# The causal mask of a stick-breaking attention: from an accumulating matmul to a table read by VectorE

## The chip, the core and the metric

The kernel runs on one core of one Trainium2 chip. The metric is device time in microseconds (us), the median of several executions. It computes two layers of a hybrid trunk on a sequence of 1024 tokens of width 1024, in float32 throughout; the large products are made of three matmuls each, of a high and a low part (`F32R`).

## The reference, cut to what matters

Each layer runs four token mixers side by side on one projection (attention, a state-space branch S5, retention, and a gated recurrence RG-LRU), gates them and projects back. The change touches the attention alone:

```python
def stick_breaking_attention(q, k, v):
    '''q, k, v: (B, H, S, d). A[t,s] = beta_ts * prod_{s<j<t} (1 - beta_tj), s < t only.'''
    ...
        z = jnp.einsum('bhqd,bhkd->bhqk', q[:, :, lo:hi], k[:, :, :hi])
        t_idx = lo + jnp.arange(Q_BLOCK)[:, None]
        s_idx = jnp.arange(hi)[None, :]
        mask = s_idx < t_idx
        log_fail = jnp.where(mask, jax.nn.log_sigmoid(-z), 0.0)
        after = lax.cumsum(log_fail, axis=3, reverse=True) - log_fail
        w = jnp.where(mask, jnp.exp(jax.nn.log_sigmoid(z) + after), 0.0)
        outs.append(jnp.einsum('bhqk,bhkd->bhqd', w, v[:, :, :hi]))
```

A weight is beta = sigmoid(z) of its own key, times the product of 1 - beta over the keys between it and the query. Keys at or after the query count as 1 in the product and get the weight 0. There are 4 heads of 64 channels and blocks of 128 queries.

## The kernel before, in words

The work is cut into four units: layer 0 and 1, and in each two halves of 512 tokens (`units`, pairs of layer l and half c). A unit is a list of 64 "tiles" of the big projections (`filler`): for each, a block of weights is loaded by DMA (`raw`), split by ScalarE (ACT) into a high part `wh` and by VectorE (DVE) into a low part `wl` (`split`, L106), and multiplied on TensorE (PE) into PSUM banks named `pa`. `ahead` splits half a tile at a time, three halves ahead of the one that PE is at; there are five buffers each for `wh` and `wl`. The projections' results are read out by ACT (sigmoid, `actv`, L83, or `copy`, L86) and DVE (`tt`, L89).

The token mixers are generators whose steps are put between the tiles by a fixed table (`PLAN`) or at fixed tiles; everything is issued in the order written, each engine works its own queue in that order, and the only thing that lets an engine go on is a semaphore. PSUM banks of the mixers are named `pb`, five in all. So PE always has projection matmuls to run between the mixers' small ones.

The attention is `sba`. It starts at tile 12 of a unit and takes two steps on every even tile. It has 16 jobs per unit: four blocks b of 128 queries, four heads h. A job's keys are cut into segments of at most 512 (`segs`): in the first half of the sequence one segment of w = 128, 256, 384 or 512 keys; in the second half one of 512 and one of 128 to 512. The last segment ends with the 128 keys of the block itself, where the mask lies. For a job i:

- first step: PE makes the logits of each segment with two matmuls (query high and low part against `kS`, L1035 and L1036). A segment of 128 keys is padded to 256 columns. In the last segment a third matmul (L1038) adds `identb` times `trib`, a 128x128 table of 0 and -1e30, to the last 128 columns: that is the mask. ACT takes two sigmoids, f = 1 - beta and `be` = beta.
- second step: DVE scans f from right to left with a running product (L1057) and multiplies `be` with it, shifted by one key. Where there are two segments, the carry goes over as `ec`, a product of two columns.
- first step of the next job: PE transposes the weights `be` in pieces of 128 (L1019), ACT copies each segment to `wt` (L86), and PE multiplies them with the values two jobs later.

The small copies to `identb` and `trib` stand in the main loop at L1439; `con` is the table of constants, loaded in `first`.

Of the kernel before, what the change touches and what calls it, by code (L numbers as in the profile page):

```python
# [24 lines left out]
EPS = 1e-6  # L25
BIG = -1e30
EXPSET = "natural_log_exp_and_others"
# [4 lines left out]

(K_ID, K_DEC, K_XI, K_ZETA, K_CD, K_TRI, NCON) = (
    0, 128, 640, 896, 900, 902, 1030)
HALF = (512, 640)
# [7 lines left out]
@with_exitstack  # L43
def hybrid_kernel(ctx: ExitStack, tc: tile.TileContext, x, xt, ws1, ws2, par, bcw, preg, postg, con, rot, out, dbg=None):
    nc = tc.nc
# [7 lines left out]
    parp = ctx.enter_context(tc.tile_pool(name="parp", bufs=1))  # L53
    smp = ctx.enter_context(tc.tile_pool(name="smp", bufs=3))
    genp = ctx.enter_context(tc.tile_pool(name="genp", bufs=NGEN))
    psa = ctx.enter_context(tc.tile_pool(name="psa", bufs=3, space=bass.MemoryType.PSUM))
# [5 lines left out]
    def nm(s):  # L62
        cnt[0] += 1
        return f"{s}{cnt[0]}"
# [60 lines left out]
    cdec = cons[:, K_CD:K_CD + 2]  # L125
    identb = const.tile([P, P], F32R, name="identb")
    trib = const.tile([P, P], F32R, name="trib")
    kS = [const.tile([P, SEQ], F32R, name=f"kS{h}") for h in range(4)]
# [215 lines left out]
    def first():  # L344
# [15 lines left out]
        load_to(3)  # L360
        sp.dma_start(cons[:, P:], con[:, P:])
        lru_load(0)

# [327 lines left out]
    def lru_load(l):  # L691
        S["lw"] = G()
        sp.dma_start(S["lw"][:, 0:256], bcw[l, :, 1024:1280])
# [194 lines left out]
    def ret(l, c):  # L888
# [70 lines left out]
        yield 0  # L959
        st = smp.tile([P, 64], F32, tag="rst", name=nm("rst"))  # L960
        mu, va, yv, av = (st[:, i * 16:(i + 1) * 16] for i in range(4))
# [27 lines left out]
    def sba(l, c):  # L989
# [9 lines left out]
        for i in range(n + 3):  # L999
# [14 lines left out]
            if 1 <= i <= n:  # L1014
                st = J[i - 1]
                for (o, w), r in zip(st["sg"], st["w"]):
                    ps = B()
                    for q in range(w // P):
                        pe.transpose(ps[:, q * P:(q + 1) * P], r[:, q * P:(q + 1) * P], ident)  # L1019
                    wt = G()  # L1020
                    copy(wt[:, 0:w], ps[:, 0:w])
                    Bdone()
                    st["wt"].append(wt)
                st["w"] = None
            if i < n:

                b, h = js[i]
                sg = segs(b)
                st = J[i] = dict(b=b, h=h, sg=sg, f=[], w=[], wt=[])
                qh, ql = S["q", b]  # L1030
                for k, (o, w) in enumerate(sg):
                    ps = B()
                    wp = max(w, 256)
                    last = k == len(sg) - 1
                    mm(ps[:, 0:wp], qh[:, h * P:(h + 1) * P], kS[h][:, o:o + wp], True, False)  # L1035
                    mm(ps[:, 0:wp], ql[:, h * P:(h + 1) * P], kS[h][:, o:o + wp], False, not last)  # L1036
                    if last:
                        mm(ps[:, w - P:w], identb, trib, False, True)  # L1038
                    f, be = G(), G()
                    actv(f[:, 0:w], ps[:, 0:w], AF.Sigmoid, scale=-1.0)  # L1040
                    actv(be[:, 0:w], ps[:, 0:w], AF.Sigmoid)
                    Bdone()
                    st["f"].append(f)
                    st["w"].append(be)
            yield 0
            if i < n:

                st = J[i]
                prev = None
                for (o, w), f, be in reversed(list(zip(st["sg"], st["f"], st["w"]))):  # L1050
                    m = w - 1
                    if prev is not None:
                        ec = smp.tile([P, 1], F32, tag="ec", name=nm("ec"))
                        tt(ec, prev[:, 0:1], prev[:, 1:2], ALU.mult)
                        tt(be[:, m:w], be[:, m:w], ec, ALU.mult)
                    fr = f[:, 1:w][:, ::-1]
                    dve.tensor_tensor_scan(out=fr, data0=fr, data1=ones1.to_broadcast([P, m]),  # L1057
                                           initial=(1.0 if prev is None else ec), op0=ALU.mult, op1=ALU.mult)
                    tt(be[:, 0:m], be[:, 0:m], f[:, 1:w], ALU.mult)
                    prev = f  # L1060
                st["f"] = None
# [364 lines left out]
    with tc.manual_schedule():  # L1426
# [9 lines left out]
        for u, (l, c) in enumerate(units):  # L1436
            for i in range(NTILE):
                if u == 0 and i == 8:
                    copy(identb, ident)  # L1439
                    copy(trib, cons[:, K_TRI:K_TRI + P])  # L1440
                if i == 12:
# [65 lines left out]
def _pack(inp):  # L1507
# [85 lines left out]
    for h in range(4):  # L1593
# [4 lines left out]
        con[64 * h2:64 * h2 + 64, K_CD + pq] = np.exp(lg[h] * f(P))  # L1598
    con[:, K_TRI:K_TRI + P] = np.where(i[None, :] >= i[:, None], f(BIG), f(0))
    inv = (f(10000.0) ** (-np.arange(32, dtype=f) / f(32))).astype(f)  # L1600
# [5 lines left out]
        "preg": np.ascontiguousarray(inp["pre_norm_g"]), "postg": np.ascontiguousarray(inp["post_norm_g"]),  # L1606
        "con": con, "rot": np.ascontiguousarray(rot),
    }
# [17 lines left out]
```

## Time and profile before

| | |
|---|---|
| median of 3 runs | 1863.25 us (1862.83 to 1863.87) |
| the profiled execution | 1862.88 us, span 1861.1 us |
| PE busy | 1826.2 us, 98% of the span |
| DVE busy | 1200.8 us, 65% |
| ACT busy | 888.2 us, 48% |
| GpSimd (POOL) busy | 258.1 us, 14% |
| granted TensorE clock, mean | 0.995 of full speed |

The profile is one execution. "Busy" is time in which at least one instruction of the engine runs; on PE the matmuls are pipelined and their recorded times overlap, so that the cost of one is read from the distance between starts. PEld is PE's weight load, which runs beside the matmuls. A name such as `pb<-kS,g` says that tile `pb` is written from `kS` and `g`; buffer numbers are left out. In square brackets stands the idle time of the engine before an instruction and what ended it.

### The profile page before, as it was taken

How to read it: one execution, taken by the hardware profiler on the slowest of the kernel's cores; microseconds unless marked ns; L12 is line 12 of the kernel's file. 1: busy time of each engine (PE TensorE's matmuls, PEld its weight loads, DVE VectorE, ACT ScalarE, POOL GpSimd, SP SyncE). 2: the span in 40 equal slices, each digit the busy share in tenths (PEclk: the TensorE clock that was granted, in tenths of full speed). 3: DMA queues.
4: the chain of work that ended last, by engine and by line, in shares of the span. 5: the costliest groups of instructions: out<-in, count | busy, mean ns of one | idle time of the engine just before them, and what ended most of it. 6: DMA issues, size and time to landing. Idle time of an engine off the chain costs nothing.

```text
span 1861.1 us, 24840 instructions
## 1 busy us (share of the span) xinstructions
PE 1826.2 (98%) x9210; PEld 1508.6 (81%) x9210; DVE 1200.8 (65%) x2168; ACT 888.2 (48%) x1673; POOL 258.1 (14%) x573
## 2 busy tenths in 40 slices
PE   9989999999999999999999999999999999999997
PEld 6767888888888888888888788888888788888886
DVE  7777755455689576744558856656437895676445
ACT  5773444344476444544546543344353845444333
POOL 6891000020000002893000000000000000000001
PEclk9999999999999999999999999999999999999999
DMA  5231232324333222232434322242243323222232
GB/s 177 99 119 48 71 125 87 125 94 154 104 132 103 89 81 71 87 135 91 145 112 136 100 90 95 78 138 99 94 139 123 118 85 102 69 78 71 99 105 102
DMA packets 68856, 193.95 MB, mean 104 GB/s; under 512 B 9600, under 2 KB 18176, under 8 KB 68736
## 3 DMA queue, kind: packets, MB, share of 16 engines
q1 hardware_dynamic: 68736, 192.38, 30.9%
q8 instruction: 72, 1.18, 0.3%
q14 instruction: 48, 0.39, 0.1%
HBM read 179.11 MB, written 12.58 MB: 103 GB/s over the span
## 4 chain that ended last, share of the span: by engine, by line
PE 85%; DVE 8%; ACT 5%; issue 1%; DMA 1%; SPq 0%; DVEq 0%; ACTq 0%
PE pa L101 66%; PE pb L101 16%; DVE g L89 2%; PE pb L1019 2%; ACT g L86 2%; ACT g L83 1%; DVE wl L89 1%; DVE g L98 1%; DVE g L93 1%; ACT wh L86 1%; DMA raw<-in_ws_dram 1%; DVE g L810 0%; PE pb L254 0%; ACT kS L86 0%; DVE g L1057 0%
## 5 line engine op out<-in xcount | busy, mean ns | idle before, releaser
L101 PE MATMUL pa<-hh,wl 128*128 128x512 f32 x1576 | 616.2, 391 | 13.3 <-DVE wl L89 13.3
L101 PE MATMUL pa<-hh,wh 128*128 128x512 f32 x1576 | 624.1, 396 | 0.1
L101 PE MATMUL pa<-hl,wh 128*128 128x512 f32 x1576 | 615.0, 390 | 0.0
L89 DVE TENSOR_TENSOR wl<-raw,wh 128x512 fp32r<-128x512 f32 (+1 forms) x512 | 374.7, 770 | 196.0 <-ACT wh L86 195.2
L89 DVE TENSOR_TENSOR g<-g,g 128x512 f32<-128x512 f32 (+7 forms) x435 | 298.8, 687 | 124.3 <-ACT g L86 104.6
L86 ACT ACTIVATE wh<-raw 128x512 fp32r<-128x512 f32 (+1 forms) x512 | 328.3, 686 | 85.6 <-PE pb L101 42.5
L101 PEld LDWEIGHTS pa<-hh,wl 128*128 128x128 f32 x1576 | 296.6, 188 | 80.0 <-DVE wl L89 16.7
L101 PEld LDWEIGHTS pa<-hh,wh 128*128 128x128 f32 x1576 | 296.7, 188 | 61.3 <-ACT wh L86 0.5
L101 PEld LDWEIGHTS pa<-hl,wh 128*128 128x128 f32 x1576 | 296.9, 188 | 58.3 <-DVE hl L89 0.2
L83 ACT ACTIVATE g<-pa 128x512 f32<-128x512 f32 x161 | 96.3, 598 | 507.1 <-PE pa L101 464.6
L89 DVE TENSOR_TENSOR g<-g,pa 128x512 f32<-128x512 f32 x128 | 87.6, 685 | 189.6 <-PE pa L101 171.2
L101 PE MATMUL pa<-g,wh 128*128 128x512 f32 x544 | 169.2, 391 | 2.4 <-ACT g L83 1.1
L905 POOL MEMSET g<- 128x512 f32 x8 | 4.0, 526 | 938.2 <-PE pb L101 937.1
L86 ACT ACTIVATE g<-pb 128x512 f32<-128x512 f32 (+4 forms) x163 | 72.8, 472 | 123.6 <-PE pb L101 88.4
L101 PEld LDWEIGHTS pa<-g,wh 128*128 128x128 f32 x544 | 102.0, 188 | 26.6 <-ACT g L83 1.9
L86 ACT ACTIVATE g<-g 128x512 fp32r<-128x512 f32 (+2 forms) x152 | 79.3, 522 | 72.6 <-DVE g L89 34.9
L101 PE MATMUL pa<-g,wl 128*128 128x512 f32 x272 | 106.0, 390 | 0.0
L83 ACT ACTIVATE g<-pb 128x512 f32<-128x512 f32 (+4 forms) x203 | 87.9, 513 | 22.4 <-PE pb L101 19.6
L86 ACT ACTIVATE g<-pa 64x128 fp32r<-64x128 f32 (+3 forms) x150 | 69.1, 461 | 34.5 <-PE pa L101 32.9
L101 PE MATMUL pa<-wh,g 128*128 128x512 f32 x256 | 79.5, 392 | 0.0
L101 PE MATMUL pb<-wh,g 128*128 128x512 f32 x256 | 79.1, 391 | 0.0
L83 ACT ACTIVATE g<-g 128x512 f32<-128x512 f32 (+2 forms) x98 | 57.1, 602 | 31.1 <-DVE g L89 22.8
(215 smaller groups left out, 2093.8 us busy)
## 6 DMA issues: line engine op xcount, KB each, us to landing
raw<-in_ws_dram SPq DMA_DIRECT2D x128, 640.0 KB, 3.9
raw<-in_ws_dram SPq DMA_DIRECT2D x127, 512.0 KB, 3.7
g<-x SPq DMA_DIRECT2D x32, 256.0 KB, 5.9
g<-in_xt_dram SPq DMA_DIRECT2D x16, 256.0 KB, 6.7
g<-in_x_dram SPq DMA_DIRECT2D x16, 256.0 KB, 3.1
x<-g SPq DMA_DIRECT2D x16, 256.0 KB, 2.1
out_dram<-g SPq DMA_DIRECT2D x16, 256.0 KB, 2.0
g<-in_rot_dram SPq DMA_DIRECT2D x8, 256.0 KB, 4.3
```

Of the source, the lines that this page charges most:

```text
L83: act.activation(out, in_, func, **kw)
L86: act.activation(out, in_, AF.Copy, **kw)
L89: dve.tensor_tensor(out, a, b, op=op)
L93: dve.tensor_scalar(out, a, s1, None, op0=op0)
L98: dve.scalar_tensor_tensor(out, in0=a, scalar=s, in1=b, op0=op0, op1=op1)
L101: pe.matmul(out, lhsT=lhsT, rhs=rhs, start=start, stop=stop)
L905: pool.memset(t, 0.0)
L1019: pe.transpose(ps[:, q * P:(q + 1) * P], r[:, q * P:(q + 1) * P], ident)
```

## The change

The mask is taken off PE. The matmul with `identb` and `trib` goes, with both tables and the copies that filled them, and so does the padding to 256 columns. In its place there is a table `tri` of 128x512 floats, 1 where a key of the block is at or after the query (in the scan's right-to-left order) and 0 elsewhere, loaded by one DMA at the start. The scan of the last segment takes `tri` as its second operand with the operation maximum: at a masked key the running product is set to 1, elsewhere it goes on. The weights of masked keys are then made 0 at the transposed side: of the last 128 columns the read-out to `wt` is a DVE multiplication with a reversed slice of `tri`, and ACT copies only the columns before them (`m` of them; none where the segment is 128 wide). The scan now covers w columns instead of w - 1, so the carry is read straight from its column 0 and `ec` is not computed. The retention's small statistics tile moves to a pool of its own with one buffer.

```diff
@@ first
         sp.dma_start(cons[:, P:], con[:, P:])
+        sp.dma_start(tri, tria)
         lru_load(0)
@@ ret
-        st = smp.tile([P, 64], F32, tag="rst", name=nm("rst"))
+        st = rsp.tile([P, 64], F32, tag="rst", name=nm("rst"))
@@ sba
                     wt = G()
-                    copy(wt[:, 0:w], ps[:, 0:w])
+                    m = w if (o, w) != st["sg"][-1] else w - P
+                    if m < w:
+                        tt(wt[:, m:w], ps[:, m:w], tri[:, 1:P + 1][:, ::-1], ALU.mult)
+                    if m:
+                        copy(wt[:, 0:m], ps[:, 0:m])
                     Bdone()
...
-                    wp = max(w, 256)
-                    last = k == len(sg) - 1
-                    mm(ps[:, 0:wp], qh[:, h * P:(h + 1) * P], kS[h][:, o:o + wp], True, False)
-                    mm(ps[:, 0:wp], ql[:, h * P:(h + 1) * P], kS[h][:, o:o + wp], False, not last)
-                    if last:
-                        mm(ps[:, w - P:w], identb, trib, False, True)
+                    mm(ps[:, 0:w], qh[:, h * P:(h + 1) * P], kS[h][:, o:o + w], True, False)
+                    mm(ps[:, 0:w], ql[:, h * P:(h + 1) * P], kS[h][:, o:o + w], False, True)
...
                     m = w - 1
-                    if prev is not None:
-                        ec = smp.tile([P, 1], F32, tag="ec", name=nm("ec"))
-                        tt(ec, prev[:, 0:1], prev[:, 1:2], ALU.mult)
+                    fr = f[:, 0:w][:, ::-1]
+                    if prev is None:
+                        dve.tensor_tensor_scan(out=fr, data0=fr, data1=tri[:, 0:w], initial=1.0, op0=ALU.mult, op1=ALU.max)
+                    else:
+                        ec = prev[:, 0:1]
                         tt(be[:, m:w], be[:, m:w], ec, ALU.mult)
-                    fr = f[:, 1:w][:, ::-1]
-                    dve.tensor_tensor_scan(out=fr, data0=fr, data1=ones1.to_broadcast([P, m]),
-                                           initial=(1.0 if prev is None else ec), op0=ALU.mult, op1=ALU.mult)
+                        dve.tensor_tensor_scan(out=fr, data0=fr, data1=ones1.to_broadcast([P, w]), initial=ec,
+                                               op0=ALU.mult, op1=ALU.mult)
                     tt(be[:, 0:m], be[:, 0:m], f[:, 1:w], ALU.mult)
@@ the main loop
-                if u == 0 and i == 8:
-                    copy(identb, ident)
-                    copy(trib, cons[:, K_TRI:K_TRI + P])
@@ _pack
-    con[:, K_TRI:K_TRI + P] = np.where(i[None, :] >= i[:, None], f(BIG), f(0))
+    tri = np.zeros((P, 512), f)
+    tri[:, 0:P] = (i[None, ::-1] >= i[:, None])
```

How the instructions stand in the queues, first on PE, at the logits of the first job (unit 0, 128 keys), before:

```order
L101 MATMUL pa_1052<-hh_439,wl_994 128x512
L101 MATMUL pb_1113<-kS_90,g_947 128x256
L101 MATMUL pb_1113<-kS_90,g_948 128x256
L101 MATMUL pb_1113<-trib,identb 128x128
L101 MATMUL pa_1125<-hh_439,wh_1009 128x512
```

and with the change:

```order
L101 MATMUL pa_1053<-hh_442,wl_995 128x512
L101 MATMUL pb_1114<-kS_92,g_948 128x128
L101 MATMUL pb_1114<-kS_92,g_949 128x128
L101 MATMUL pa_1125<-hh_442,wh_1010 128x512
L101 MATMUL pa_1125<-hl_442,wh_1010 128x512
```

The matmul with `trib` is gone from all 64 jobs, and 32 matmuls of 16 jobs are 128 instead of 256 columns wide; nothing else moves on PE.

The second place is ACT's and DVE's queue at the read-out of the transposed weights of unit 0's last job (512 keys); the last bracket names the engines whose semaphores an instruction waits for. ACT before:

```order
L83 ACTIVATE g_3315<-pa_3273 128x512 [waits PE_49]
L86 ACTIVATE g_3324<-pb_3319 128x512 [waits PE_49]
L86 ACTIVATE wh_3329<-raw_3226 128x640 [waits DVE_49]
L86 ACTIVATE wh_3348<-raw_3274 128x512 [waits DMAHW4_49,DVE_49]
L83 ACTIVATE g_3368<-pa_3326 128x512 [waits PE_49]
```

ACT with the change:

```order
L83 ACTIVATE g_3311<-pa_3269 128x512 [waits PE_49]
L86 ACTIVATE g_3320<-pb_3315 128x384 [waits DVE_49]
L86 ACTIVATE wh_3326<-raw_3222 128x640 [waits Activation_49]
L86 ACTIVATE wh_3345<-raw_3270 128x512 [waits DMAHW5_49,Activation_49]
L83 ACTIVATE g_3365<-pa_3323 128x512 [waits PE_49]
```

and DVE with the change:

```order
L89 TENSOR_TENSOR g_3311<-g_3311,pa_3304 128x512 [waits PE_49,Activation_49]
L89 TENSOR_TENSOR g_2076<-g_2076,g_3311 128x512 [waits DVE_49]
L89 TENSOR_TENSOR g_3320<-pb_3315,tri 128x128 [waits PE_49]
L89 TENSOR_TENSOR wl_3327<-raw_3222,wh_3326 128x640 [waits Activation_49]
L89 TENSOR_TENSOR wl_3346<-raw_3270,wh_3345 128x512 [waits DMAHW5_49,Activation_49]
```

ACT's copy is 128 columns shorter and waits for DVE instead of PE; on DVE the multiplication with `tri` is new, behind the two operations on the projection's result and ahead of the next two `wl` splits. Of the 64 read-outs 48 have such an ACT copy and all 48 wait for DVE; the other 16 (128 keys in the last segment) have the DVE multiplication alone.

## Rows read from the trace of the kernel before

**Rows 1.** The page, busy time of PE and its weight load.
```profile
PE 1826.2 (98%) x9210; PEld 1508.6 (81%) x9210; DVE 1200.8 (65%) x2168; ACT 888.2 (48%) x1673; POOL 258.1 (14%) x573
```

**Rows 2.** Busy time by stretch: start:end, length, engines, PE clock, DMA share, GB/s.
```profile
170.00:550.00 380.00, 380.00 (x1845) 315.59 (x1845) 231.13 (x409) 171.80 (x314) 11.69 (x10) 1.00 0.33 111
550.00:600.00 50.00, 48.07 (x236) 38.95 (x235) 48.41 (x96) 34.01 (x71) 0.00 (x0) 1.00 0.27 90
600.00:1000.00 400.00, 399.48 (x2130) 332.78 (x2129) 246.87 (x426) 192.84 (x355) 113.61 (x274) 1.00 0.31 102
...
1040.00:1460.00 420.00, 420.00 (x2071) 348.31 (x2071) 252.46 (x459) 183.54 (x342) 0.99 (x2) 1.00 0.33 110
1460.00:1510.00 50.00, 48.10 (x237) 38.98 (x237) 46.90 (x92) 38.18 (x81) 0.00 (x0) 1.00 0.30 101
1510.00:1861.00 351.00, 339.13 (x1786) 281.97 (x1784) 210.21 (x376) 141.59 (x258) 8.50 (x8) 0.99 0.26 87
```

**Rows 3.** The same view of the mask's matmuls alone (tile trib), PE and PEld.
```profile
170.00:550.00 380.00, 2.67 (x12) 2.25 (x12) 0.00 (x0) 1.00 0.33 111
600.00:1000.00 400.00, 2.68 (x12) 2.26 (x12) 0.00 (x0) 1.00 0.31 102
1030.00:1460.00 430.00, 3.35 (x15) 2.81 (x15) 0.00 (x0) 1.00 0.33 110
1510.00:1861.00 351.00, 2.69 (x12) 2.26 (x12) 0.00 (x0) 0.99 0.26 87
```

**Rows 4.** Timeline of PE at the first job: start, length, what, count.
```profile
81.62 0.39 PE L101 MATMUL pa<-hh,wl 128*128 128x512 f32 x1
81.85 0.40 PE L101 MATMUL pb<-kS,g 128*128 128x256 f32 x2
82.09 0.23 PE L101 MATMUL pb<-trib,identb 128*128 128x128 f32 x1
82.15 0.45 PE L101 MATMUL pa<-hh,wh 128*128 128x512 f32 x1
82.43 0.40 PE L101 MATMUL pa<-hl,wh 128*128 128x512 f32 x1
```

**Rows 5.** Groups of DVE by form: count, busy us and mean ns.
```profile
L1057 DVE TENSOR_TENSOR_SCAN g<-g,ones 128x511 f32<-128x511 f32 x16 | 19.7, 1228 | 0.0
...
L89 DVE TENSOR_TENSOR g<-g,ec 128x1 f32<-128x1 f32 x32 | 5.3, 165 | 1.2
...
L89 DVE TENSOR_TENSOR ec<-g 128x1 f32<-128x1 f32 x32 | 5.2, 161 | 0.0
L754 DVE TENSOR_TENSOR_SCAN g<-g,lcar,g 128x512 f32<-128x512 f32 x4 | 5.1, 1284 | 0.1
...
L89 DVE TENSOR_TENSOR g<-g,g 128x127 f32<-128x127 f32 x16 | 4.7, 293 | 0.6
```

**Rows 6.** Timeline of ACT at the read-out of unit 0's last job.
```profile
346.68 0.60 ACT L83 ACTIVATE g<-pa 128x512 f32<-128x512 f32 x1 [4.92 <-PE pa L101]
348.49 0.60 ACT L86 ACTIVATE g<-pb 128x512 f32<-128x512 f32 x1 [1.20 <-PE pb L1019]
348.98 1.25 ACT L86 ACTIVATE wh<-raw 128x640 fp32r<-128x640 f32 x2
```

**Rows 7.** Timeline of DVE at the same place.
```profile
348.12 0.69 DVE L89 TENSOR_TENSOR g<-g,pa 128x512 f32<-128x512 f32 x1 [3.92 <-PE pa L101]
348.84 0.69 DVE L89 TENSOR_TENSOR g<-g,g 128x512 f32<-128x512 f32 x1
349.74 1.43 DVE L89 TENSOR_TENSOR wl<-raw,wh 128x640 fp32r<-128x640 f32 x2 [0.21 <-ACT wh L86]
```

**Rows 8.** Timeline of ACT, then DVE, at the seventh job's read-out in unit 0.
```profile
210.56 1.34 ACT L86 ACTIVATE g<-pb 128x512 f32<-128x512 f32 x3 [1.64 <-PE pb L982]
...
217.35 0.60 ACT L83 ACTIVATE g<-pa 128x512 f32<-128x512 f32 x1 [3.74 <-PE pa L101]
...
214.36 0.68 DVE L983 COPY g<-pb 128x512 f32<-128x512 f32 x1
```

**Rows 9.** The chain that ended last, at the start: one issue on SP's queue.
```profile
3.54 0.43 SPq L351
```

More of the change, by code (lines that the diff above doesn't have):

```diff
@@ L25 @@
 EPS = 1e-6
-BIG = -1e30
 EXPSET = "natural_log_exp_and_others"
@@ L31 @@
     0, 8, 10, 12, 14, 16, 18, 26, 34, 42, 50, 58)
-(K_ID, K_DEC, K_XI, K_ZETA, K_CD, K_TRI, NCON) = (
-    0, 128, 640, 896, 900, 902, 1030)
+(K_ID, K_DEC, K_XI, K_ZETA, K_CD, NCON) = (
+    0, 128, 640, 896, 900, 902)
 HALF = (512, 640)
@@ L43, in hybrid_kernel @@
 @with_exitstack
-def hybrid_kernel(ctx: ExitStack, tc: tile.TileContext, x, xt, ws1, ws2, par, bcw, preg, postg, con, rot, out, dbg=None):
+def hybrid_kernel(ctx: ExitStack, tc: tile.TileContext, x, xt, ws1, ws2, par, bcw, preg, postg, con, tria, rot, out, dbg=None):
     nc = tc.nc
@@ L54, in hybrid_kernel @@
     smp = ctx.enter_context(tc.tile_pool(name="smp", bufs=3))
+    rsp = ctx.enter_context(tc.tile_pool(name="rsp", bufs=1))
     genp = ctx.enter_context(tc.tile_pool(name="genp", bufs=NGEN))
@@ L125, in hybrid_kernel @@
     cdec = cons[:, K_CD:K_CD + 2]
-    identb = const.tile([P, P], F32R, name="identb")
-    trib = const.tile([P, P], F32R, name="trib")
+    tri = const.tile([P, 512], F32, name="tri")
     kS = [const.tile([P, SEQ], F32R, name=f"kS{h}") for h in range(4)]
@@ L1606, in _pack @@
         "preg": np.ascontiguousarray(inp["pre_norm_g"]), "postg": np.ascontiguousarray(inp["post_norm_g"]),
-        "con": con, "rot": np.ascontiguousarray(rot),
+        "con": con, "tri": tri, "rot": np.ascontiguousarray(rot),
     }
```

## The prediction

> **What bounds the kernel now.** I read the page first, then busy time by stretch. On the page PE is busy for 1826.2 us [rows 1], 35 us less than the span of 1861.1, and DVE for 1200.8. An average hides which engine is late where, so the second view matters more. From 170 to 550, 600 to 1000, 1040 to 1460 and from 1510 to the end PE is busy all the time (380.00 of 380, 399.48 of 400, 420.00 of 420; the last stretch ends with the final output), with DVE at 231 of 380 and ACT at 172 of 380 [rows 2]. There each nanosecond taken from PE is one off the end. From 550 to 600 and from 1460 to 1510 it is otherwise: PE lacks 2 us in each, and DVE is at 48.41 and 46.90 of 50 [rows 2]. In these, the first jobs of the units in the second half of the sequence, DVE sets the pace. The start, up to 170, and the stretch around 1030 also have waits of PE for DVE.
>
> **The change, part by part.**
>
> *The mask's matmul goes.* Its recorded 0.23 us is not its price, since matmuls overlap. I take the distance between starts. In the projection before it, one matmul follows another after 0.23 us (81.62 to 81.85). The mask starts at 82.09 and the matmul behind it at 82.15, so its own distance is 0.06; but that next one then takes 0.28 (82.15 to 82.43) instead of 0.23 [rows 4]. Together 0.34 stand where 0.23 would: 0.11 us per job. The Trainium skill, TensorE: Matmul & The Clock Gate, "Wait — 56ns, not 53.3ns?", has consecutive matmuls of 128 columns 55.6 ns apart at the full clock, which is the first of the two distances and leaves out the second. By it the gain would be about half, an estimate of 51 x 0.056 = 2.9 us. I go by both distances of the row, since the second is there only behind the mask.
>
> How many of the 64 count? Those in stretches where PE waits for nothing: 12, 12, 15 and 12, in all 51 [rows 3]. The other 13 stand ahead of a wait of PE for DVE; what PE saves there it spends in that wait, and I count nothing. 51 x 0.11 = 5.6 us saved. Ends: 51 x 0.06 = 3.1 if the second distance stays, 64 x 0.11 = 7.0 if the 13 count too.
>
> *Logits of 128 keys are not padded.* 32 matmuls go from 256 to 128 columns. The two padded ones need 0.24 together (81.85 to 82.09), 0.12 each [rows 4]. The nearest row for a narrow one of the same kind is the mask itself: 0.06 plus the 0.05 it adds to the next. So 0.01 each, 0.3 us for all; 0.1 taken, since half of them stand where PE waits. Ends: 32 x 0.06 = 1.9 us saved if only the mask's own distance counts; 32 x (0.23 - 0.12) = 3.5 us lost if a narrow one cost what one of 512 columns does, against which the mask's short record (0.23 beside 0.39) speaks.
>
> *DVE's multiplications with the table.* 64 new ones of 128x128. Nearest row: 0.293 us for 128x127 from SBUF [rows 5]. That is 18.8 us of DVE. Gone are 32 `ec` products of 0.161 us, 5.2 us [rows 5]. In the four stretches where PE is full this hides in DVE's idle time, 149 us in the first alone [rows 2]. In the two where DVE sets the pace it counts: three multiplications fall ahead of PE's last wait, 0.88, less three to four `ec`, 0.5 to 0.6, so 0.3 us each and 0.6 in all. In the first jobs of the first unit there is nothing to take off, but ACT loses a copy there; zero taken, 1 us kept as an end.
>
> *The scan reads a table.* 1.228 us with a constant operand, 1.284 where both operands are full tables (the recurrence's scan) [rows 5]. At most 0.06 x 64 = 3.6 us of DVE, and less for shorter ones; zero on the path, by the same idle time.
>
> *ACT waits for DVE.* This is the wait that the change adds. The order shows that ACT's copy of the unmasked columns now waits for DVE's multiplication, 48 times. Behind that copy, on ACT, stand the sigmoids of the next logits and the next two `wh` splits; for those wait DVE's `wl` splits, and for both PE. At unit 0's last job ACT starts its copy at 348.49 [rows 6]. DVE has work until 348.84 + 0.69 = 349.53 [rows 7], and 0.29 more for the multiplication makes 349.82: ACT starts 1.3 us later, and its copy is 0.1 shorter. So the splits come 1.2 us later. The worst place I found is the seventh job of unit 0: DVE is in a run of small operations until 214.36 + 0.68 = 215.04, where ACT had ended its copies at 211.90 (210.56 + 1.34) [rows 8]; there it is 3.8 us. The cover: the splits are made three halves ahead, a half is 12 to 15 projection matmuls of 0.23, so 8 to 10 us, of which a pair of splits needs 1.25 + 1.43 [rows 6, 7]; about 5 us stay. That the cover is real shows in what ACT and DVE wait for: PE, for 4.92 and 3.92 us ahead of this job [rows 6, 7], and for 3.74 us right after the seventh job [rows 8]. I take zero; if all of it came through it would be 47 x 1.2 + 3.8 = 60 us.
>
> *DVE waits for the transposes.* It comes to them after ACT did (349.53 against 348.49), so it rarely waits. Zero.
>
> *The rest.* One more DMA of 256 KB on SP's queue ahead of the recurrence's weights: 0.43 us of issue [rows 9], behind four weight tiles that are already under way; zero taken, 0.5 us as an end. The shorter constants, the two copies gone and the pool of one buffer, used once per unit, cost nothing.
>
> **Sum.** -5.6 - 0.1 + 0.6 = -5.1 us. The profiled execution took 1862.88 us, which gives 1857.8; the median of the runs is 0.4 above it, which gives 1858.2. I say 1858.0 us, 0.3% faster. A measurement of this kernel can tell about 0.2%, 3.7 us, from no change, so "faster" ends at 1859.5.
>
> **The rivals.**
>
> *A: only the mask's own 0.06 us comes back.* The next matmul keeps its 0.28 because its weights, and not the mask, are late. For it: weight load is busy for 1508.6 us [rows 1]. Against: elsewhere the projection runs at 0.23 with the same loads. 51 x 0.06 = 3.1, less 0.6 on DVE: 1860.6 us, no difference that can be told. The Trainium skill's distance named above would make it so. Chance 0.11.
>
> *B: ACT's new wait reaches PE, and the kernel gets slower.* The place is the 48 read-outs, the price 1.2 us each and 3.8 at the run of small operations, and the point is where the delay exceeds the lead of the splits. Of the 60 us exposed, 5.1 reaching PE cancel the gain; if a fifth does, 12 us, the time is 1863.1 + 6.9 = 1870 us. For it: two engines now wait in turn in one queue order, several times per unit. Against: the idle times named. The Trainium skill, PSUM — Partial Sum Buffer, "Terms", says that two engines may not access the same bank in the same partitions at once, reads included; the two read-outs of one bank therefore cannot overlap, and the order here has them one behind the other. Chance 0.08.
>
> *C: DVE's extra work counts wherever PE waits.* The 13 jobs outside the full stretches pay 0.29 each and get nothing for `ec`: 3.8 us, -5.6 + 3.8 = -1.8, so 1861.3 us. For it: DVE at 48.41 of 50 [rows 2]. Against: half of these jobs lose an `ec`, and ACT gets shorter. Chance 0.09.
>
> *D: all 64 jobs count, and the narrow logits gain too.* 7.0 + 1.9 = 8.9 us: 1854.2 us. It needs the waits for DVE to shrink with PE's work, for which little speaks. Chance 0.14.
>
> The change could also fail to do what it says if a narrow matmul were dear; that is the 3.5 us above and 1861.5 us, and its small chance is in C's.
>
> **How the numbers follow.** Forecast 0.58 (1856 to 1859.5, its unknowns: 0.5 us of DMA, 1 us on DVE at the start), A 0.11, B 0.08, C 0.09, D 0.14. Faster: 0.58 + 0.14 = 0.72; same: A and C, 0.20; slower: B, 0.08. The range from 1854.0 to 1862.5 leaves out B and the far ends, under 2 in 10.
>
> **What would show it.** Right: 64 fewer PE matmuls; behind logits of 256 columns or more the projection's second matmul follows its first after 0.23 instead of 0.28; the four full stretches shorter by 1.3 to 1.7 us each and still without a wait of PE; ACT's copies up to 4 us after the transposes, and no new wait of PE for `wl`. Wrong: waits of PE for `wl` or `wh` between 170 and 550 (B), waits of the transposes for DVE growing by over 0.3 us (C), those second matmuls still 0.28 behind the first (A), narrow logits further apart than 0.12.

## The result, and the profile after

| kernel | median | runs |
|---|---|---|
| before | 1862.88 us (1859.91 to 1863.87) | 6 |
| with the change | 1878.65 us (1874.44 to 1878.98) | 6 |

The ratio is 1.0082, 95% interval 1.0071 to 1.0093: the changed kernel is slower by 15.8 us. The forecast was 1858.0 us, its range ended at 1862.5, and "slower" had been given 0.08. The profiled execution took 1878.98 us, its span is 1877.2 us.

The first line to look at is the busy time on the page of the changed kernel, beside [rows 1]:

```profile
PE 1839.9 (98%) x9146; PEld 1505.7 (80%) x9146; DVE 1212.1 (65%) x2200; ACT 881.2 (47%) x1655; POOL 260.0 (14%) x573
```

PE has 64 instructions fewer and is busy 13.7 us longer. The span grew by 16.1 us, so most of the loss doesn't stand where a new wait would show, in PE's idle time. It is inside the time in which PE works. The view by stretch says the same, beside [rows 2]:

```profile
170.00:550.00 380.00, 380.00 (x1819) 312.55 (x1819) 231.87 (x419) 167.33 (x304) 11.73 (x10) 0.99 0.32 109
550.00:600.00 50.00, 47.98 (x233) 38.45 (x232) 47.08 (x93) 36.40 (x77) 0.00 (x0) 1.00 0.29 100
600.00:1000.00 400.00, 397.89 (x2094) 327.97 (x2093) 243.76 (x418) 184.74 (x340) 115.48 (x274) 1.00 0.29 100
1040.00:1460.00 420.00, 420.00 (x2040) 344.78 (x2040) 255.05 (x467) 177.76 (x331) 0.99 (x2) 1.00 0.32 108
```

From 170 to 550 and from 1040 to 1460 PE is still busy all the time, yet it gets through 26 and 31 instructions fewer than before. Only 12 and 14 of these are the missing mask matmuls (the fifteenth of [rows 3] stands before 1040), and in the first stretch a part is the granted clock, 0.99 instead of 1.00. From 600 to 1000 1.6 us of idle time have come on top. So there are two things to find: matmuls that follow one another more slowly, and a small new wait.

The groups of PE by form tell which matmuls. Columns are count, busy us and mean ns of one, then the idle time ahead of them. Before:

```profile
L101 PE MATMUL pa<-hh,wh 128*128 128x512 f32 x1576 | 624.1, 396 | 0.1
L101 PE MATMUL pa<-g,wh 128*128 128x512 f32 x544 | 169.2, 391 | 2.4 <-ACT g L83 1.1 <-DVE g L98 0.6 <-ACT wh L86 0.5
L101 PE MATMUL pa<-wh,g 128*128 128x512 f32 x256 | 79.5, 392 | 0.0
L101 PE MATMUL pb<-wl,g 128*128 128x512 f32 x128 | 49.8, 389 | 0.0
```

The same groups with the change:

```profile
L101 PE MATMUL pa<-hh,wh 128*128 128x512 f32 x1576 | 624.0, 396 | 0.0
L101 PE MATMUL pa<-g,wh 128*128 128x512 f32 x544 | 174.6, 400 | 5.6 <-ACT g L86 2.1 <-DVE g L89 1.7 <-ACT g L83 1.2
L101 PE MATMUL pa<-wh,g 128*128 128x512 f32 x256 | 80.8, 397 | 0.0
L101 PE MATMUL pb<-wl,g 128*128 128x512 f32 x128 | 50.8, 397 | 0.0
```

A name after the arrow gives the moving operand first and the weights second. The projection of `hh` is as fast as before. Every one of these groups that reads a general tile `g` is slower, as moving operand (`g,wh`) or as weights (`wh,g`). The change touches neither the instructions nor the shapes of these groups, and most of them are far from the attention. The plainest place is a run of 192 such matmuls (`wh` and `wl` with `g`) in the first unit, in which PE waits for nothing. First and last of it on PE's timeline, before:

```profile
431.07 0.71 PE L101 MATMUL pa<-wh,g 128*128 128x512 f32 x2
...
474.46 0.39 PE L101 MATMUL pa<-wl,g 128*128 128x512 f32 x1
```

and with the change:

```profile
433.16 0.71 PE L101 MATMUL pa<-wh,g 128*128 128x512 f32 x2
...
477.81 0.39 PE L101 MATMUL pa<-wl,g 128*128 128x512 f32 x1
```

191 distances take 43.39 us before and 44.65 with the change: 227.2 and 233.8 ns each. With the clock at full speed and the same shapes, what can differ is the place of the tiles; it follows from the declarations. The tiles of SBUF lie one behind another as the program declares them, each rounded up to 32 bytes per partition. The diff moves them: `cons` is 512 bytes shorter, `identb` and `trib` (1024) are gone, `tri` (2048) is new, so all that follows lies 512 higher; the statistics tile `rst` has one buffer of 256 bytes instead of three, and the three buffers of `ec` (96) are gone. The tiles `g` come last and begin 96 bytes lower than before, at byte 155488 of a partition instead of 155584; `wh` begins 512 bytes higher, at 128704 instead of 128192. The distance from `wh` to `g` was 27392 bytes, 107 times 256, and is 26784, 104 times 256 and 160.

### The profile page after: what moved, and what is told of

The parts are those of the page before. It is cut to its first block, busy times and chain, and to the rows that moved or that the text cites. A ratio compares the mean times of both kernels' runs of the same rounds, so it can differ in the third digit from the quotient of the medians.

```text
span 1877.2 us, 24679 instructions
## 1 busy us (share of the span) xinstructions
PE 1839.9 (98%) x9146; PEld 1505.7 (80%) x9146; DVE 1212.1 (65%) x2200; ACT 881.2 (47%) x1655; POOL 260.0 (14%) x573
## 4 chain that ended last, share of the span: by engine, by line
PE 79%; DVE 9%; POOL 6%; ACT 3%; issue 2%; DMA 1%; SPq 0%; DVEq 0%; POOLq 0%; ACTq 0%
PE pa L101 62%; PE pb L101 14%; DVE g L89 3%; POOL g L431 2%; PE pb L1019 2%; DVE wl L89 2%; DVE g L98 1%; ACT g L83 1%; POOL psc L435 1%; ACT g L86 1%; POOL ptmp L431 1%; DVE g L93 1%; ACT wh L86 1%; POOL tsin L431 0%; POOL tcos L431 0%
## 5 line engine op out<-in xcount | busy, mean ns | idle before, releaser
L101 PE MATMUL pa<-hh,wl 128*128 128x512 f32 x1576 | 619.3, 393 | 12.1 <-DVE wl L89 11.9
L86 ACT ACTIVATE wh<-raw 128x512 fp32r<-128x512 f32 (+1 forms) x512 | 329.3, 684 | 91.4 <-PE pb L101 45.9
L101 PE MATMUL pa<-g,wh 128*128 128x512 f32 x544 | 174.6, 400 | 5.6 <-ACT g L86 2.1
L86 ACT ACTIVATE g<-pb 128x512 f32<-128x512 f32 (+4 forms) x147 | 66.7, 459 | 164.9 <-PE pb L101 87.3
L86 ACT ACTIVATE g<-g 128x512 fp32r<-128x512 f32 (+2 forms) x152 | 79.1, 521 | 73.5 <-DVE g L89 36.7
L83 ACT ACTIVATE g<-pb 128x512 f32<-128x512 f32 (+4 forms) x203 | 87.4, 504 | 23.4 <-PE pb L101 19.3
L86 ACT ACTIVATE g<-pa 64x128 fp32r<-64x128 f32 (+3 forms) x150 | 69.0, 460 | 36.1 <-PE pa L101 34.1
```

The costliest lines, as they stand in the source:

```text
L83: act.activation(out, in_, func, **kw)
L86: act.activation(out, in_, AF.Copy, **kw)
L101: pe.matmul(out, lhsT=lhsT, rhs=rhs, start=start, stop=stop)
```

## The experiments

Two theories. **Layout**: the slower matmuls come from where `g` lies. **Wait**: rival B of the prediction, the 48 waits of ACT for VectorE. The first can be tested without moving one instruction, by the size of one small tile.

**1. Moving g alone.** In the changed kernel, `rst` is made 32 bytes longer (e1_align):

```diff
-        st = rsp.tile([P, 64], F32, tag="rst", name=nm("rst"))
+        st = rsp.tile([P, 72], F32, tag="rst", name=nm("rst"))
```

In the kernel before, an unused tile of 32 bytes is put ahead of `g` (e2_shift):

```diff
+    padt = parp.tile([P, 8], F32, tag="padt", name="padt")
     genp = ctx.enter_context(tc.tile_pool(name="genp", bufs=NGEN))
```

> The changed kernel with the normalisation's small tile rst declared 72 instead of 64 columns wide, 32 bytes more per partition, so that the general tiles g start 32 bytes later, on a multiple of 64 bytes as in the kernel before (their first byte is 155520 = 2430 x 64; in the changed kernel 155488, in the one before 155584 = 2431 x 64). No instruction differs. Theory L (layout): in the changed kernel the 512-column matmuls that read a tile g, as weights or as moving operand, follow one another after 232 to 237 ns in place of 227, which sums to 16.4 us; back on 64 bytes they take 227 again and the time falls from 1878.7 to 1862 us, or to about 1857 if the 5 us that the longer stretches at the lower clock cost go too. Theory W (waits, rival B of the prediction): the loss comes from ACT's wait for the VectorE multiplication, which a shift of 32 bytes does not touch: 1875 to 1879 us.

> The kernel before with one unused tile of 32 bytes per partition declared ahead of the general tiles, which moves every tile g to 32 bytes past a multiple of 64; hh, hl, wh, wl and kS stay where they were and no instruction differs. Theory L: the matmuls on g slow to 232 to 237 ns and the kernel takes 1862.9 + 16.4 = 1879 us (1876 to 1881). Theory W: 1862.9 us, as before.

Measured: 1869.2 us (ratio to before 1.0041, 1.0027 to 1.0055) and 1871.05 us (1.0049, 1.0037 to 1.0062). The second makes the kernel before 9.3 us slower with 32 unused bytes, so the layout has a price; the run of 192 takes 233.7 ns a piece in it. The 16.4 us that both expectations count with was too much, and 1876 to 1881 us was missed: summed over the 1632 matmuls of 512 columns between `g` and `wh` or `wl` (those that follow another of 512 columns within 0.26 us), the distances are 9.4 us longer than in the kernel before, in e2_shift and in the changed kernel alike. The first gave back a part, and its numbers refute the form of the theory: `g` lay on a multiple of 64 bytes again, and still its matmuls stood at 229.4 in the run of 192, and at 233 (median distance) with `g` as moving operand and `wh` as weights.

**2. The mask's matmul, and the padding, by themselves.** On the kernel before, the third matmul goes, and nothing masks the block of 128 keys (e3_nomask):

```diff
-                    mm(ps[:, 0:wp], ql[:, h * P:(h + 1) * P], kS[h][:, o:o + wp], False, not last)
-                    if last:
-                        mm(ps[:, w - P:w], identb, trib, False, True)
+                    mm(ps[:, 0:wp], ql[:, h * P:(h + 1) * P], kS[h][:, o:o + wp], False, True)
```

On e1_align, the padding comes back (e4_pad), in both matmuls; that widens 32 matmuls, not the 64 of its expectation:

```diff
+                    wp = max(w, 256)
-                    mm(ps[:, 0:w], qh[:, h * P:(h + 1) * P], kS[h][:, o:o + w], True, False)
+                    mm(ps[:, 0:wp], qh[:, h * P:(h + 1) * P], kS[h][:, o:o + wp], True, False)
```

> The kernel before without its 64 mask matmuls and with nothing in their place (the causal mask inside the diagonal block is left out); every tile stays where it was. It prices the prediction's first term alone: 51 of 64 at 0.11 us are -5.6 us, so 1857.3 us; by the matmul's own 0.06 us alone (rival A) -3.8 with all 64, so 1859.1; if nearly all of it lay in waits, 1862.9.

> e1_align with the 64 logits matmuls of 128 keys widened to 256 again. It prices the second term: taken as -0.1 us for the narrow form, so e1_align + 0.1; the ends of the range were -1.9 (the narrow one costs its own columns alone) and +3.5 us (it is dearer), so from e1_align + 1.9 down to e1_align - 3.5.

Measured: 1857.12 us without the mask (0.9971, 0.996 to 0.9983), 4.6 us off by the medians and 5.4 by the ratio; 1870.31 with the padding (1.0049, 1.0036 to 1.0062), against 1869.2 without it, intervals overlapping. The times don't speak against either term; the distances say more. PE's timeline at unit 0's last job, before:

```profile
334.11 0.22 PE L101 MATMUL pb<-trib,identb 128*128 128x128 f32 x1
334.17 0.45 PE L101 MATMUL pa<-hh,wh 128*128 128x512 f32 x1
334.45 0.40 PE L101 MATMUL pa<-hl,wh 128*128 128x512 f32 x1
```

and in e3_nomask:

```profile
332.55 0.71 PE L101 MATMUL pb<-kS,g 128*128 128x512 f32 x2
333.10 0.40 PE L101 MATMUL pa<-hh,wh 128*128 128x512 f32 x1
333.33 0.40 PE L101 MATMUL pa<-hl,wh 128*128 128x512 f32 x1
```

The second projection matmul follows the first after 0.23, not 0.28. The narrow logits of the first job, in the changed kernel:

```profile
81.25 0.33 PE L101 MATMUL pb<-kS,g 128*128 128x128 f32 x2
81.42 0.45 PE L101 MATMUL pa<-hh,wh 128*128 128x512 f32 x1
81.70 0.39 PE L101 MATMUL pa<-hl,wh 128*128 128x512 f32 x1
```

The two take 0.17 and the matmul behind them 0.28, together 0.45; padded they took 0.24 [rows 4], and with 0.23 behind them that is 0.47. So a job saves 0.02 us here.

**3. Alike within what?** `hh`, `hl`, `wh` and `wl` all lay 192 bytes past a multiple of 256 so far. Three more placements, all on the changed kernel: `rst` 88 columns wide, which puts `g` exactly where it was in the kernel before (e8_same); 64 unused bytes ahead of all other tiles, and `rst` 72, so that `g` stays there (e9_w64); the same with `g` moved as well (e10_all64). The last two are:

```diff
+    padt = const.tile([P, 16], F32, name="padt")
     hp = ctx.enter_context(tc.tile_pool(name="hp", bufs=1))
...
-        st = rsp.tile([P, 64], F32, tag="rst", name=nm("rst"))
+        st = rsp.tile([P, 72], F32, tag="rst", name=nm("rst"))
```

```diff
+    padt = const.tile([P, 16], F32, name="padt")
     hp = ctx.enter_context(tc.tile_pool(name="hp", bufs=1))
...
-    smp = ctx.enter_context(tc.tile_pool(name="smp", bufs=3))
+    smp = ctx.enter_context(tc.tile_pool(name="smp", bufs=2))
...
-        st = rsp.tile([P, 64], F32, tag="rst", name=nm("rst"))
+        st = rsp.tile([P, 80], F32, tag="rst", name=nm("rst"))
```

> The changed kernel with rst declared 88 instead of 64 columns wide, 96 bytes more per partition: the general tiles g begin at byte 155584, the very address they had in the kernel before (64 past a multiple of 128, as hh, hl, wh and wl are in all kernels so far; in e1_align they began on a multiple of 128). No instruction differs. Theory L128 (what counts is the place within 128 bytes): the matmuls on g, which still took 230 to 233 ns in e1_align where they stand at 227 in the kernel before, take 227 again, which is 9 us off e1_align's 1869.2: 1860 us, and below the kernel before by the mask's 4.6 us less the new waits of about 2 us. Theory W (what e1_align left is the wait of ACT for the multiplication and not the layout): 1869 us as e1_align.

> As e8_same, with g at byte 155584, but an unused tile of 64 bytes ahead of everything else moves hh, hl, wh, wl and the constants from 64 past a multiple of 128 to a multiple of 128. Theory absolute (a tile has to lie 64 past a multiple of 128): the 4700 matmuls of hh and hl with wh and wl slow by about 6 ns, 28 us: 1885 us or more, those on g partly stay at 227. Theory relative (moving operand and weights have to lie alike within 128 bytes): only the matmuls of g with wh and wl slow, as in e1_align: 1869 us. Theory W: 1869 us, with no spacing changed.

> As e9_w64, and g moved too, to a multiple of 128 (byte 155392; the small tiles' pool has two buffers instead of three, to make the room): hh, hl, wh, wl and g lie alike again, all 64 bytes away from where they lie in e8_same. Theory relative: 1860 us as e8_same, all spacings 227. Theory absolute: every 512-column matmul slows by about 6 ns, 1890 us or more.

Measured: 1864.07 us (1.0009, 1.0000 to 1.0018), 1871.52 (1.0045, 1.0032 to 1.0059) and 1864.24 (1.0004, 0.9995 to 1.0013). The first and the last are 4 us above the 1860 that was expected, though the distances in the table below are back at 227; what is left is in experiment 4. The absolute theory is out: moving `hh` and `wh` together leaves their own matmuls at 227. What counts is how far moving operand and weights lie apart. One more run asks for the period (e13_256: `smp` with two buffers, `rst` 112 wide); it stands on e11_copyfirst of experiment 4, whose time with `g` well placed is 1858.7:

> e11_copyfirst with g moved down by 128 bytes, to byte 155456 (the small tiles' pool has two buffers instead of three, as in e10_all64): still 64 past a multiple of 128, but no longer like hh, wh and wl within 256 bytes (64 against 192). If being alike within 128 bytes is what counts: 227 ns for the matmuls on g and 1858.7 us. If it is 256: 230 to 237 ns, and 1867 to 1869 us.

Measured: 1864.52 us (1.0023, 1.0013 to 1.0033); the median distances of the groups with `g` and `wh` or `wl` are 231 to 237, so 128 is not enough. The time is below the 1867 to 1869 us that were expected for this: four of its nine executions took 1868.0 to 1868.7 us and five 1863.5 to 1864.5. The profiled one is of the lower group, and its mean granted clock from 60 to 200 us is 0.99, where e11_copyfirst's is 0.95. An estimate from this: 0.04 of 140 us are 5.6 us. So what the clock does at the start can hide half of the layout's price in a time; the distances show it. All eight layouts, by the run of 192 (191 distances, from the timeline, as above):

| bytes from `wh` to `g`, remainder by 256 | kernel | ns each |
|---|---|---|
| 0 | before; e8_same; e10_all64 | 227.2; 227.2; 227.3 |
| 32 | e2_shift | 233.7 |
| 128 | e13_256 | 233.7 |
| 160 | with the change | 233.8 |
| 192 | e1_align; e9_w64 | 229.4; 229.4 |

In e8_same the run stands on PE's timeline as it did before the change:

```profile
430.15 0.71 PE L101 MATMUL pa<-wh,g 128*128 128x512 f32 x2
...
473.54 0.39 PE L101 MATMUL pa<-wl,g 128*128 128x512 f32 x1
```

The logits' own matmuls of 512 columns, `kS` with `g`, stood at a median of 235 to 239 in the runs so far, and from `kS` to `g` it is 32 bytes over a multiple of 256 in the kernel before and in e8_same. Putting the 32-byte tile `lcar` ahead of `kS` places it like `g`, in the kernel before (e7_ks_before) and in e11_copyfirst (e12_best).

```diff
+    lcar = const.tile([P, 2], F32, name="lcar")
     kS = [const.tile([P, SEQ], F32R, name=f"kS{h}") for h in range(4)]
...
-    lcar = const.tile([P, 2], F32, name="lcar")
```

> The kernel before with lcar declared ahead of kS, so that kS lies like g within 128 bytes (both 64 past a multiple); nothing else moves but vsb and uext by 32 bytes. Theory relative: the 96 logits matmuls of 512 columns go from 238 to 227 ns (-1.0 us), the narrower ones save a little: 1860.6 us against 1862. Without an effect of layout on them: 1862.

> e11_copyfirst with the declaration of one tile of 32 bytes (lcar) moved ahead of kS, so that kS begins 64 past a multiple of 128 as g, hh, hl, wh and wl do, in place of 32 past it. The 512-column logits matmuls (moving operand kS, weights g) stand at 236 to 238 ns in every run so far, where like-placed pairs stand at 227. Theory relative: the 96 of them go to 227 (-0.9 us) and the 384- and 256-column ones save about 5 ns each (-0.5 us): 1857.3 us against e11_copyfirst's 1858.7. If the 236 ns belong to the logits for another reason: 1858.7.

Measured: 1861.73 (1.0003, 0.9994 to 1.0012) and 1858.43 us (0.9984, 0.9975 to 0.9992), and the medians stay at 235 and 236. This was a miss, and the median misled: it mixes two kinds. In every run 38 of the 96 stand right behind the transposes of 128 columns and have a median of 314 to 319 ns to the next; that is seen above, in the 0.55 us that two logits matmuls take together in e3_nomask. The other 58 have a median of 230 to 234. In these, placing `kS` like `g` changed 232 to 231 (e7_ks_before) and left it at 232 (e12_best), so 227 wasn't reached; why is open.

**4. ACT's wait.** With `g` well placed, e8_same is still 6 to 7 us above what the mask's price promises (1862.09 - 4.6 = 1857.5). Two ways to take the wait away, both on e8_same. ACT copies the whole block and VectorE multiplies in place (e11_copyfirst):

```diff
                     m = w if (o, w) != st["sg"][-1] else w - P
-                    if m < w:
-                        tt(wt[:, m:w], ps[:, m:w], tri[:, 1:P + 1][:, ::-1], ALU.mult)
-                    if m:
-                        copy(wt[:, 0:m], ps[:, 0:m])
+                    copy(wt[:, 0:w], ps[:, 0:w])
+                    if m < w:
+                        tt(wt[:, m:w], wt[:, m:w], tri[:, 1:P + 1][:, ::-1], ALU.mult)
```

Or ACT's copy is simply written ahead of the multiplication (e14_swap):

```diff
-                    if m < w:
-                        tt(wt[:, m:w], ps[:, m:w], tri[:, 1:P + 1][:, ::-1], ALU.mult)
                     if m:
                         copy(wt[:, 0:m], ps[:, 0:m])
+                    if m < w:
+                        tt(wt[:, m:w], ps[:, m:w], tri[:, 1:P + 1][:, ::-1], ALU.mult)
```

> e8_same, but ACT copies the whole block of transposed weights out of PSUM first, as in the kernel before, and VectorE then multiplies the diagonal 128 columns in place in SBUF by the table: ACT waits for VectorE no more. If ACT's wait has a price (rival B of the prediction, in small: two new gaps of 1.04 and 0.55 us on PE at 678 and two at 1598 us in e1_align, 3.2 us together), e8_same less 2 to 3 us; if those gaps belong to something else, as e8_same within 0.5 us; dearer if ACT's 16 additional copies and longer ones (about 13 us of ACT work) count, e8_same plus up to 1 us.

> e8_same with ACT's copy written ahead of VectorE's multiplication, both still out of PSUM and each on its own columns: ACT waits for VectorE no more, VectorE waits for ACT instead, and no work is added or taken away. Theory wait (e11_copyfirst's gain of 5.4 us over e8_same is the 48 waits of ACT that are gone): 1858 to 1860 us. Theory port (it is the VectorE's read of the PSUM tile that e11_copyfirst takes away): 1864 us as e8_same.

Measured: 1858.68 us (0.9976, 0.9968 to 0.9985) and 1857.68 us (0.9973, 0.9964 to 0.9982). The first is 5.4 us below e8_same, more than the 2 to 3 expected. The second changes only the order of two instructions in the program, and it is as fast: the wait is the cause, not the reading of PSUM by VectorE. In all, the waits of ACT at L86 for VectorE grew with the change. The view of ACT's waits (us in total, times, longest), before:

```profile
ACT g L86 <- DVE g L89: 34.9, 28, 6.8
```

and with the change:

```profile
ACT g L86 <- DVE g L89: 90.4, 63, 5.9
```

In e14_swap they are at 36.3 again. Of the 90.4 us, 53.6 were spent behind the multiplications with `tri`, at 38 of the 48 copies. Where it hurts shows in the changed kernel at about 675 (the same comes again at about 1603, one layer later). The timeline of ACT there:

```profile
676.60 0.60 ACT L86 ACTIVATE g<-pb 128x512 f32<-128x512 f32 x1
680.91 0.28 ACT L86 ACTIVATE g<-pb 128x128 f32<-128x128 f32 x1 [3.71 <-DVE g L89]
681.09 1.85 ACT L83 ACTIVATE g<-pb 128x512 f32<-128x512 f32 x4
682.78 1.39 ACT L86 ACTIVATE wh<-raw 128x640 fp32r<-128x640 f32 x2
684.04 0.66 ACT L86 ACTIVATE g<-g 128x512 fp32r<-128x512 f32 x1
```

The timeline of DVE at the same place:

```profile
674.27 3.71 DVE L98 SCALAR_TENSOR_TENSOR g<-g,cons,pb 64x64 f32<-64x64 f32 x12
678.01 1.22 DVE L98 SCALAR_TENSOR_TENSOR rcar<-g,cons,pb 64x64 f32<-64x64 f32 x4
679.26 0.69 DVE L89 TENSOR_TENSOR g<-pa,g 128x512 f32<-128x512 f32 x1
679.99 0.69 DVE L89 TENSOR_TENSOR g<-g,g 128x512 f32<-128x512 f32 x1
680.60 0.28 DVE L89 TENSOR_TENSOR g<-pb,tri 128x128 f32<-128x128 f32 x1
```

and that of PE:

```profile
684.75 0.50 PE L101 MATMUL pa<-g,wh 128*128 128x512 f32 x1 [1.07 <-ACT g L86]
685.80 0.50 PE L101 MATMUL pa<-g,wh 128*128 128x512 f32 x1 [0.56 <-DVE g L89]
```

ACT stands 3.71 us behind the retention's run of small operations on DVE. Behind its copy are four sigmoids, two weight splits and then `g<-g`, the split of a mixer's gated output, which PE multiplies with `wh` next. PE waits 1.07 and 0.56 us. Then the granted clock falls. In the view by stretch of the changed kernel, the third number from the end is the clock:

```profile
680.00:684.00 4.00, 3.68 (x17) 2.69 (x15) 1.29 (x3) 3.09 (x7) 0.00 (x0) 1.00 0.00 0
684.00:686.20 2.20, 0.90 (x3) 0.48 (x3) 2.20 (x4) 1.81 (x4) 0.00 (x0) 1.00 0.38 74
686.50:689.50 3.00, 3.00 (x19) 2.61 (x19) 2.93 (x6) 0.57 (x1) 0.00 (x0) 0.50 0.36 145
690.00:694.00 4.00, 4.00 (x20) 3.26 (x19) 3.79 (x6) 0.00 (x0) 0.00 (x0) 1.00 0.00 0
```

The clock is at 0.50, the 1.2 of the two levels 1.2 and 2.4 GHz, from about 686.2 to 689.6, right behind the gaps; an estimate of what that costs is half of the 3.4 us, 1.7. So a place costs up to 3.3 us, two of them 6.6. The trace of the changed kernel has the lower clock behind both places, that of e1_align behind the first alone, those of e8_same and e16_after_again (experiment 5) behind the second alone. In e14_swap the timeline of ACT has at this place:

```profile
672.04 0.77 ACT L86 ACTIVATE g<-pb 128x512 f32<-128x512 f32 x2
672.69 1.86 ACT L83 ACTIVATE g<-pb 128x512 f32<-128x512 f32 x4
...
676.16 0.63 ACT L86 ACTIVATE g<-g 128x512 fp32r<-128x512 f32 x1 [0.37 <-DVE g L89]
```

and that of PE, behind it:

```profile
678.30 0.62 PE L101 MATMUL pa<-g,wh 128*128 128x512 f32 x2
...
678.99 0.61 PE L101 MATMUL pa<-g,wh 128*128 128x512 f32 x2
```

Here ACT's copies don't wait for DVE, and PE doesn't wait at all: the split of the gated output ends at 676.79 and PE takes it at 678.99. So its lead is about 2.2 us even here. The multiplication comes when DVE is free.

**5. Do the two causes add up?** The four corners, on one chip. e15_swap_only has the order of e14_swap and `rst` 64 wide; the other three are the changed kernel, e8_same and e14_swap as they were.

> The changed kernel with ACT's copy written ahead of VectorE's multiplication (as e14_swap), and the tiles g left where the change put them (byte 155488, 96 below the place they have in the kernel before and in e8_same, where they lie like hh, wh and wl within 256 bytes). The fourth corner of two causes. If layout and wait add up: e14_swap's 1857.7 plus the 9 to 11 us that the misplaced g costs, 1867 to 1869 us, and the 5 to 6 us of the wait below the changed kernel's 1878.7 are 1873, so the two ways must not meet: a remainder of up to 5 us would be something that the two causes make together.

> The changed kernel unchanged, beside its variants on one chip, since the runs so far compare it with them over different chips and its six runs fell into two groups (1874.4 to 1875.0 and 1878.6 to 1879.0). Expected 1875 to 1879 us. Layout and wait adding up from e14_swap make 1857.7 + 9.3 (e2_shift) + 6.4 (e8_same less e14_swap) = 1873.4 us.

> e8_same unchanged (layout mended, wait left), on the same chip: 1864 us, 9 to 15 us below the changed kernel.

> e14_swap unchanged (layout mended, wait gone), on the same chip: 1858 us, 5 to 6.5 us below e17_same_again and about 4 us below the kernel before; the version that beats both kernels.

| | ACT waits for DVE | ACT copies first |
|---|---|---|
| `g` 96 off | e16_after_again, 1876.71 (1.0075, 1.0062 to 1.0087) | e15_swap_only, 1868.91 (1.0037, 1.0024 to 1.0049) |
| `g` as before | e17_same_again, 1865.11 (1.0008, 0.9999 to 1.0017) | e18_swap_again, 1857.97 (0.9977, 0.9967 to 0.9986) |

Layout: 1868.91 - 1857.97 = 10.9 us, or 11.6 in the other column. Wait: 1865.11 - 1857.97 = 7.1 us, or 7.8 in the other row. Together with the change's own gain (1857.97 - 1862.29 = -4.3): 1862.29 - 4.3 + 10.9 + 7.1 = 1876.0, against 1876.71 measured. They add up to within 0.7 us, where each ratio's interval is about 2 us to either side, so no third thing is needed. (The 1873.4 us in the expectation of e16_after_again put the two prices at 9.3 and 6.4 us, and was too low.) The 14.6 us that e8_same seemed to give for the layout (1878.65 - 1864.07) compares runs on different chips; on one it is 11.6. The traces of e15_swap_only and e18_swap_again have the same instructions, so their distances on PE can be compared one by one: of 10.6 us between them, 9.3 lie on the 1632 matmuls between `g` and `wh` or `wl` (5.7 ns each), 0.9 on the matmul right behind such a one, and 3.1 on the 4800 or so of `hh` and `hl` (0.6 ns each; why is open), while gaps and stretches at the lower clock are 2.7 shorter.

The trace of e17_same_again, an execution of 1860.95 us, shows the gaps on PE but no fall of the clock behind them:

```profile
677.02 0.49 PE L101 MATMUL pa<-g,wh 128*128 128x512 f32 x1 [1.05 <-ACT g L86]
678.08 0.50 PE L101 MATMUL pa<-g,wh 128*128 128x512 f32 x1 [0.56 <-DVE g L89]
```

```profile
678.00:688.00 10.00, 9.92 (x68) 7.95 (x70) 8.88 (x15) 1.41 (x3) 0.00 (x0) 1.00 0.34 114
```

So the clock's part of the wait's price comes and goes between executions.

## Why the prediction was wrong

Point by point, in its own order.

*The mask's matmul: right.* -5.6 us forecast, 4.6 measured alone (the interval is 3.2 to 7.4). What would show it was there: the 0.23 behind the logits of 256 columns or more, and 64 matmuls fewer. The time alone wouldn't exclude rival A, which gives 3.8 us if all 64 count; the distances do. Rival A is out with them, and so is the sum by the distance that the Trainium skill gives (TensorE: Matmul & The Clock Gate, "Wait — 56ns, not 53.3ns?"): the matmul cost its own 0.06 and the 0.05 on the next, as [rows 4] said. At the 16 last segments of 512 keys, the distance from the last logits matmul to the first projection matmul had a median of 291 ns with the mask and 232 without, and the next one 285 and 231: 113 ns together.

*The narrow logits: not contradicted.* -0.1 us forecast; putting the padding back changed nothing that can be told, and the 0.02 us per job seen in the timeline agrees with the 0.01 per matmul that was worked out.

*DVE's multiplications, the scan with a table: right.* The 64 multiplications take 18.2 us of DVE (0.284 each; 0.293 taken), and with the rest in order the kernel reaches 1857.97 and 1857.68, where the forecast's sum said 1857.8 to 1858.2. That it is so close is in part luck: against the kernel before of the same rounds it is 4.3 and 4.2 us, and the sum said 5.1, inside the intervals. No term of the sum need be missing there. The multiplications waited for the transposes, which the forecast had at zero, 11 times and 10.5 us in all on DVE, without a cost that shows.

*"I take zero" for ACT's wait: failed.* The exposure was sized well: ACT's waits for DVE at L86 grew by 90.4 - 34.9 = 55.5 us, where the prediction had 60. The worst place that it named, the seventh job of the first unit, got a wait of 3.99 us where it said 3.8 (the rows that it shows make 215.04 + 0.29 - 211.90 = 3.4). The chain behind the wait was followed too short. It went from ACT's copy to the weight splits, and found a cover of about 5 us in the three halves of lead. That cover held: PE's waits for `wl` went from 13.5 to 12.1 us, and PE has no wait at all from 170 to 550, the seventh job included. But the same ACT queue also holds the split of the gated outputs (`g<-g`), which has a lead of only about 2.2 us even in e14_swap. There 3.71 us of ACT's wait became 1.63 of PE's, twice, and in some executions the clock's fall came on top; 7.1 us in all by the medians. Rival B was right in kind; its price, 12 us at a fifth of 60, was too high and its place (the splits' lead) wrong. The Trainium skill's rule in that rival (PSUM — Partial Sum Buffer, "Terms") played no part that a run shows: with the same two read-outs of one bank in the other order the loss was gone.

*"The rest ... cost nothing": failed, and this is the larger part.* "The shorter constants, the two copies gone and the pool of one buffer" were costed as work, and as work they are nothing. But with the new table they are also what moved `wh` up by 512 bytes and `g` down by 96, and this cost 10.9 us, most of it on the 1632 matmuls of 512 columns between `g` and `wh` or `wl`. No rival of the prediction had it, and the range had no room for it. The diff held all that was needed to work out the new places, but no row of the trace of before held the price: it has only the good case, 227 ns, and `kS`, whose median of 238 turned out to be something else.

## What to carry to other kernels

When a change adds, drops or resizes any tile, write down where the big tiles lie before and after. Here `g` and `wh` or `wl` had to lie a multiple of 256 bytes apart. If groups that the change doesn't touch slow down, move them back with a small pad and measure that first, and read the price from the distances of one long run: the times also carry what the clock does elsewhere. When an engine gets a new wait, follow everything in its queue behind the wait to the consumer with the least lead, in each kind of unit, and not only the one that feeds the main loop. Where two engines read parts of one tile, try both orders; here it paid to let the one with the fuller queue behind it go first.

The version that beats both kernels is e14_swap, the changed one with two edits: `rst` 88 columns wide, and ACT's copy ahead of the multiplication. It takes 1857.68 us (0.9973, 0.9964 to 0.9982) and, a second time, 1857.97 (0.9977, 0.9967 to 0.9986).

## What the runs showed of the hardware that was not expected

- 512-column float32 matmuls follow one another after 227.2 ns when moving operand and weights lie a multiple of 256 bytes apart, after 229.4 at a remainder of 192, and after 233.7 to 233.8 at 32, 128 and 160. These numbers are with `g` as weights; with `g` as moving operand and `wh` as weights the medians are 227 against 231 to 235, and 233 at a remainder of 192 too. Where both are moved alike (e10_all64) nothing changes. What in the hardware does this wasn't tried, nor were other remainders or types.
- It was not seen for `kS` with `g`: away from the transposes, 231 and 232 ns when alike, 232 when 32 off.
- A matmul of 512 columns right behind short ones keeps the next waiting longer: 285 ns to the next behind the mask, 231 without it, and 314 to 319 for the logits behind the transposes, 230 to 234 elsewhere.
- Behind two gaps of about 1.07 and 0.56 us on PE the granted clock stood at 0.50 for 3.4 us in some executions; in others it stayed at 1.00. Without the gaps (e11_copyfirst, e14_swap) it stayed at 1.00 there.
